# Weight chunks whose low parts come from an accumulating transfer, in a two-layer decoder trunk

## The chip, the cores and the metric

One core of one Trainium2 chip runs the whole program. The metric is the device time of one execution in microseconds (us). Before the change it is 446.27 us, the median of three runs (446.05 to 446.99).

## The reference

`reference` sends x (256 rows of 1024 numbers) through two layers, each closed by `x <- LayerNorm(alpha * x + sublayer(x))`:

```python
h = x @ w_in                                            # layer 0: retention and latent attention
rq, rk, rv, rg, mq, mkv, mkr, mg = _split(h, EVEN_SPLITS)
o_r = head_group_norm(retention_chunkwise(q_r, k_r, _heads(rv, RET_HEADS)))
ret_out = (_merge(o_r) * jax.nn.silu(rg.astype(jnp.float32))).astype(x.dtype)
q_m = rms_norm(mq, q_norm_g) @ w_uq                     # heads are split off in between
kv = rms_norm(mkv, kv_norm_g) @ w_ukv
o_m = causal_attention(q_full, k_full, v_m, (MLA_NOPE + MLA_ROPE) ** -0.5)
return jnp.concatenate([ret_out, mla_out], axis=-1) @ w_out
...
h = x @ w_in                                            # layer 1: block-sparse attention
return (_merge(o) * jax.nn.silu(g)) @ w_out
```

All of it is float32. There are 4 retention heads, 8 latent-attention heads and 16 heads in layer 1, and nearly all of the arithmetic is in the products with the weights.

## The kernel before

**Three matrix multiplications for one.** A float32 product is made of fast multiplications on rounded operands. Each operand is split into a high part, the operand rounded, and a low part, the rest. `mm3` (L169 to L173) then multiplies high by high (L171), low by high (L172 or L173, by which operand comes first) and high by low. The names of parts end in _h or _hi and in _l or _lo.

**Weight chunks.** The weights are cut into 138 chunks in the order in which they are used (`PLAN`); this text counts them from 0, as the code's `state["u"]` does. `fetch` (L190) loads the next chunk from the queue of SP (L195) into a buffer called raw, one of a ring of four, and `load` (L200) has it split by `wsplit` (L204) and `split_to` (L175): ScalarE (ACT in the profile) writes the high part w_h by a copy that rounds (L176), and VectorE (DVE) writes the low part w_l = raw - w_h (L177). There are six buffers for w_h and six for w_l, and raw is free again when the subtraction is done. Chunks 0 to 8 also carry columns of x, transposed, and four of these lie in the ring, five in other buffers. From chunk 9 on nearly all are 128x1024 (512 KB). GpSimd (POOL) does only a few powers for the norms.

**Order.** The order of TensorE (PE) is written out by hand, as tasks that are put between the products of the weights. The other engines stand in an order that a scheduler worked out when the program was built. A load counts its landing on one of eight counters (DMAHW0 to DMAHW7) that are given out in turn, and an instruction that issues a transfer first waits until the counter's previous transfer has landed. Two loads that are not of weights are issued from ACT's queue between its copies for the first chunks (L280): the constants cs, and the retention decay, called decay.

**Places that the prediction speaks of.** Chunk 5 is one of the first nine, whose products go to pm. Chunk 16 is a value chunk of the first retention head (pv). Chunks 88 to 93 lie around the end of the last gate product of layer 0 (pg, gated by L423 and L424 into rgate) and the start of its output projection (acc). The high part of chunk 93 lies in a buffer of its own, w_rqk_h. Chunk 104 is a value chunk of layer 1 (pvo). Chunks 136 and 137 are the last two, of the output projection of layer 1; around them the attention of the last heads is finished: ppt (L566) holds probabilities transposed by PE, which ACT and DVE split into pT_h and pT_l for the product poc, and cog (L840) is the gated result, split into oT_h and oT_l for the output projection acc.

Of the kernel before, what the change touches and what calls it, by code (L numbers as in the profile page):

```python
# [9 lines left out]
F32 = mybir.dt.float32  # L10
F32R = mybir.dt.float32r
BF16 = mybir.dt.bfloat16
I32 = mybir.dt.int32
AF = mybir.ActivationFunctionType
OP = mybir.AluOpType
AX = mybir.AxisListType

P = 128
S = 256
NT = S // P  # L20
DM = 1024
# [10 lines left out]
WBUFS = 6  # L32
# [10 lines left out]
VAL = 1, 2, 1, 1  # L43
LAT1, LAT2, QR = 5, 1, 7
WARM = 9

OFF = np.cumsum([0, 1024, 1024, 2048, 2048, 256, 256, 64, 1024])
O_RQ, O_RK, O_RV, O_RG, O_MQ, O_MKV, O_MKR, O_MG = [int(v) for v in OFF[:8]]
# [106 lines left out]
def trunk(ctx, tc, x, lng, lnb, w, cst, dec, out):  # L155
    nc = tc.nc
    cp = ctx.enter_context(tc.tile_pool(name="const", bufs=1))
    wp = ctx.enter_context(tc.tile_pool(name="weights", bufs=1))
    even = ctx.enter_context(ExitStack())
    wk = even.enter_context(tc.tile_pool(name="even", bufs=1))  # L160
# [5 lines left out]
    def at(name):  # L166
        return ps.tile([P, 512], F32, name=name, tag="at", bufs=4)
# [7 lines left out]
    def split_to(hi, lo, src):  # L175
        done = nc.scalar.activation(hi, src, AF.Copy)  # L176
        nc.vector.tensor_tensor(lo, src, hi.bitcast(F32), op=OP.subtract)  # L177
        return done

    def split(src, shape, name, pool=None, tag=None, bufs=1):  # L180
        pool = pool or wk
        tag = tag or name
        hi = pool.tile(shape, F32R, name=name + "_h", tag=tag + "_h", bufs=bufs)
        lo = pool.tile(shape, F32R, name=name + "_l", tag=tag + "_l", bufs=bufs)
        split_to(hi, lo, src)
        return hi, lo

    state = {"u": 0, "off": 0, "tick": 0}

    def fetch(name, extra=0, home=None):  # L190
        tag, _, ks, cols = PLAN[state["u"]]
        assert tag == name, (tag, name)
        n = len(ks) * len(cols) + extra
        raw = wk.tile([P, n], F32, name="raw", tag=home) if home else wp.tile([P, n], F32, name="raw", tag="raw", bufs=4)
        nc.sync.dma_start(raw, bass.AP(tensor=w.tensor, offset=w.offset + state["off"], ap=[[n, P], [1, n]]))  # L195
        state["u"] += 1
        state["off"] += n * P
        return raw, n, ks, cols

    def load(name, tags=None, raw=None):  # L200
        raw, n, ks, cols = raw or fetch(name)
        return ks, [t.rearrange("p (k c) -> p k c", c=len(cols)) for t in wsplit(raw, n, tags)]

    def wsplit(raw, n, tags):  # L204
        if not tags:
            return split(raw, [P, n], "w", wp, "w", WBUFS)
        hi, lo = [wk.tile([P, n], F32R, name="w_" + t, tag=t) for t in tags]
        split_to(hi, lo, raw)
        return hi, lo
# [36 lines left out]
    pidle = at("pidle")  # L246
    for _ in range(WARM):
        nc.tensor.matmul(pidle, idle[:, :P], idle, start=True, stop=True)
# [21 lines left out]
    xn = [cp.tile([P, DM], F32, name=f"xn{t}") for t in range(NT)]  # L270
    homes = [None] * 4 + [n + e for n in ("rqk", "mqk", "rv") for e in ("_h", "_l")]
    first = [fetch("m", 0 if i == 1 else S, homes[i]) for i in range(KD + 1)]
    for i, (raw, n, ks, cols) in enumerate(first):
        k = ks[0]
        if i != 1:
            at_act = split_to(xT_hi[:, k, :], xT_lo[:, k, :], raw[:, :S])
            for at_k, dst, src in ((2, cs, cst), (4, decay, dec)):
                if k == at_k:
                    with tc.issue_after(at_act.ins):
                        nc.scalar.dma_start(dst, src)  # L280
        wv = wsplit(raw[:, n - len(cols):], len(cols), None)
        for i2 in range(len(cols) // 288):
            j = max(i2, int(i == 1))
            for t in range(NT):
                mm3(pm[t][j][:, :288], x_rows(k), wv, lambda z: z[:, t * P:(t + 1) * P],
                    lambda z: z[:, i2 * 288:(i2 + 1) * 288], start=k == 0, stop=k == KD - 1)
# [19 lines left out]
    for bits in (2.0 ** -2, 2.0 ** -5, 2.0 ** -15, 2.0 ** -22):  # L306
        c = math.floor(rest / bits) * bits
# [89 lines left out]
    def block_proj(name, lhs, tiles, nk=KD):  # L397

        done = 0
        while done < nk:  # L400
            ks, wv = load(name)
            for i, k in enumerate(ks):
                for t in range(NT):
                    mm3(tiles[t], lhs(k), wv, lambda z: z[:, t * P:(t + 1) * P], lambda z: z[:, i, :],
                        start=done == 0, stop=done == nk - 1)
                done += 1
            tick()

    def blockT_proj(name, o):

        ov = o.rearrange("p (c s) -> p c s", c=2)
        for _ in range(2):
            ks, wv = load(name)
            for i, k in enumerate(ks):
                for c in range(2):
                    mm3(ov[:, c, :], wv, x_rows(k), lambda z: z[:, i, c * P:(c + 1) * P], lambda z: z,
                        start=k == 0 and c == 0, stop=k == KD - 1)
            tick()
# [21 lines left out]
    def retention(h, mid=None):  # L440
# [3 lines left out]
        for _ in range(KD // 2):  # L444
            ks, wv = load("qk")
            for i, k in enumerate(ks):
                for c in range(4):
                    mm3(v4[c // 2][:, c % 2, :], wv, x_rows(k), lambda z: z[:, i, c * P:(c + 1) * P],
                        lambda z: z, start=k == 0 and c % 2 == 0, stop=k == KD - 1)
            tick()  # L450
# [331 lines left out]
    wk = ctx.enter_context(tc.tile_pool(name="odd", bufs=1))  # L782
# [87 lines left out]
    for n in range(len(held), 8):  # L870
        if "turned" in state:
            with tc.issue_after(state.pop("turned").ins):
                ks, wv = load("v")
        else:
            ks, wv = load("v")
# [3 lines left out]
    for i in range(2):  # L879
        hi, lo = [wk.tile([P, NT, 512], F32R, name=f"cv{i}_{e}") for e in "hl"]  # L880
# [79 lines left out]
```

## Time and profile before

| | |
|---|---|
| median of three runs | 446.27 us |
| the profiled execution: its time / its span | 447.49 us / 445.7 us |
| PE busy with matrix multiplications / loading weights | 436.2 us (98%) / 389.9 us (87%) |
| DVE busy | 329.9 us (74%) |
| ACT busy | 247.3 us (55%) |
| POOL busy | 10.9 us (2%) |
| mean granted clock of PE | 0.945 of full speed |
| weights' queue: bytes, share of the 16 DMA engines' span | 70.66 MB, 49.6% |
| chain of work that ended last | PE 92%, DVE 3%, ACT 2%, DMA 1%, issue 1% |

The span runs from the first instruction to the last. An engine's busy time is the time in which one of its instructions runs, and it says nothing by itself about whether another engine waits for it: that is read from the waits and from single instructions in the timeline.

### The profile page before, as it was taken

How to read it: one execution, taken by the hardware profiler on the slowest of the kernel's cores; microseconds unless marked ns; L12 is line 12 of the kernel's file. 1: busy time of each engine (PE TensorE's matmuls, PEld its weight loads, DVE VectorE, ACT ScalarE, POOL GpSimd, SP SyncE). 2: the span in 40 equal slices, each digit the busy share in tenths (PEclk: the TensorE clock that was granted, in tenths of full speed). 3: DMA queues.
4: the chain of work that ended last, by engine and by line, in shares of the span. 5: the costliest groups of instructions: out<-in, count | busy, mean ns of one | idle time of the engine just before them, and what ended most of it. 6: DMA issues, size and time to landing. Idle time of an engine off the chain costs nothing.

```text
span 445.7 us, 7654 instructions
## 1 busy us (share of the span) xinstructions
PE 436.2 (98%) x2959; PEld 389.9 (87%) x2959; DVE 329.9 (74%) x586; ACT 247.3 (55%) x439; POOL 10.9 (2%) x18
## 2 busy tenths in 40 slices
PE   8999999999999999999999999999999999999993
PEld 6998899988998888889998888888899999999883
DVE  4889789785876866556488569668767698889747
ACT  5777456663556543345465755503645868595810
POOL 0020000000000000000000000000000000000001
PEclk9999999999999999999999999999999999999997
DMA  8977545454463566554646557922866354634002
GB/s 283 347 242 246 188 143 183 148 168 141 143 188 109 181 203 220 162 189 145 211 142 189 178 176 226 304 63 85 273 207 190 97 169 125 185 96 137 1 1 94
DMA packets 21780, 75.55 MB, mean 170 GB/s; under 512 B 2416, under 2 KB 2800, under 8 KB 21744
## 3 DMA queue, kind: packets, MB, share of 16 engines
q1 hardware_dynamic: 20304, 70.66, 49.6%
q10 hardware_dynamic: 1440, 4.41, 2.9%
q8 instruction: 23, 0.38, 0.3%
q14 instruction: 13, 0.11, 0.1%
HBM read 74.01 MB, written 1.05 MB: 168 GB/s over the span
## 4 chain that ended last, share of the span: by engine, by line
PE 92%; DVE 3%; ACT 2%; DMA 1%; issue 1%; SPq 0%; DVEq 0%; ACTq 0%
PE pg L171 5%; PE pg L172 5%; PE pg L173 5%; PE pj L171 4%; PE pv L171 3%; PE pj L172 3%; PE pj L173 3%; PE pv L173 3%; PE pv L172 3%; PE acc L171 3%; PE acc L172 3%; PE acc L173 3%; PE pa L172 3%; PE pa L173 3%; PE pa L171 2%; PE pq L171 2%
## 5 line engine op out<-in xcount | busy, mean ns | idle before, releaser
L177 DVE TENSOR_TENSOR w_l<-raw,w_h 128x1024 fp32r<-128x1024 f32 (+3 forms) x134 | 156.4, 1170 | 55.1 <-ACT w_h L176 53.7
L176 ACT ACTIVATE w_h<-raw 128x1024 fp32r<-128x1024 f32 (+3 forms) x134 | 135.5, 1015 | 94.9 <-PE pa L172 19.3
L171 PE MATMUL pj<-xT_hi,w_h 128*128 128x256 f32 x128 | 36.1, 282 | 0.0
L172 PE MATMUL pj<-xT_hi,w_l 128*128 128x256 f32 x128 | 35.8, 279 | 0.0
L173 PE MATMUL pj<-xT_lo,w_h 128*128 128x256 f32 x128 | 35.7, 279 | 0.0
L171 PE MATMUL pv<-w_h,xT_hi 128*128 128x512 f32 x64 | 25.7, 402 | 0.0
L171 PE MATMUL pg<-w_h,xT_hi 128*128 128x512 f32 x64 | 25.7, 402 | 0.0
L172 PE MATMUL pg<-w_h,xT_lo 128*128 128x512 f32 x64 | 25.3, 395 | 0.0
L172 PE MATMUL pv<-w_h,xT_lo 128*128 128x512 f32 x64 | 25.3, 395 | 0.0
L173 PE MATMUL pv<-w_l,xT_hi 128*128 128x512 f32 x64 | 25.3, 395 | 0.0
L173 PE MATMUL pg<-w_l,xT_hi 128*128 128x512 f32 x64 | 25.2, 395 | 0.0
L171 PEld LDWEIGHTS pj<-xT_hi,w_h 128*128 128x128 f32 x128 | 24.0, 188 | 0.5
L172 PEld LDWEIGHTS pj<-xT_hi,w_l 128*128 128x128 f32 x128 | 24.0, 188 | 0.0
L173 PEld LDWEIGHTS pj<-xT_lo,w_h 128*128 128x128 f32 x128 | 24.0, 187 | 0.0
L171 PE MATMUL pq<-xT_hi,w_h 128*128 128x256 f32 x64 | 18.3, 286 | 0.0
L171 PE MATMUL pg<-xT_hi,w_h 128*128 128x256 f32 x64 | 18.1, 283 | 0.0
L171 PE MATMUL pmg<-xT_hi,w_h 128*128 128x256 f32 x64 | 18.1, 282 | 0.0
L171 PE MATMUL pkk<-xT_hi,w_h 128*128 128x256 f32 x64 | 18.0, 281 | 0.0
L173 PE MATMUL pmg<-xT_lo,w_h 128*128 128x256 f32 x64 | 17.9, 279 | 0.0
L173 PE MATMUL pkk<-xT_lo,w_h 128*128 128x256 f32 x64 | 17.9, 279 | 0.0
L172 PE MATMUL pq<-xT_hi,w_l 128*128 128x256 f32 x64 | 17.9, 279 | 0.0
L173 PE MATMUL pq<-xT_lo,w_h 128*128 128x256 f32 x64 | 17.9, 279 | 0.0
(302 smaller groups left out, 1239.1 us busy)
## 6 DMA issues: line engine op xcount, KB each, us to landing
raw<-w SPq DMA_DIRECT2D x125, 512.0 KB, 3.8
raw<-w SPq DMA_DIRECT2D x7, 416.0 KB, 7.1
raw<-w SPq DMA_DIRECT2D x4, 256.0 KB, 2.7
xn<-x ACTq DMA_DIRECT2D x2, 512.0 KB, 4.2
decay<-dec ACTq DMA_DIRECT2D x1, 512.0 KB, 7.2
decay_ln<-lng ACTq DMA_DIRECT2D x1, 512.0 KB, 4.1
rv_h_ln<-lnb ACTq DMA_DIRECT2D x1, 512.0 KB, 3.7
lng_ln<-lng ACTq DMA_DIRECT2D x1, 512.0 KB, 4.0
```

The lines of the kernel that those rows point to most:

```text
L171: nc.tensor.matmul(o, ca(a[0]), cb(b[0]), start=start, stop=False, skip_group_check=True)
L172: nc.tensor.matmul(o, ca(a[1]), cb(b[0]), start=False, stop=False, skip_group_check=True)
L173: state["mm"] = nc.tensor.matmul(o, ca(a[0]), cb(b[1]), start=False, stop=stop, skip_group_check=True)
L176: done = nc.scalar.activation(hi, src, AF.Copy)
L177: nc.vector.tensor_tensor(lo, src, hi.bitcast(F32), op=OP.subtract)
```

## The change

For every fourth chunk from chunk 16 on that has 1024 columns and takes the ordinary buffers (26 of the 138: 16, 20, 28, 32, 36, 44, 48, 52, 56, 60, 64, 72, 80, 84, 88, 92, 100, 104, 108, 112, 116, 120, 124, 128, 132, 136), DVE no longer subtracts. ACT writes two copies of raw, the high part and its negative (into the low part's buffer), and a transfer issued by POOL adds raw onto the negative, which leaves raw - w_h there. The ring of raw has five buffers in place of four, and the program reserves 4096 bytes for descriptors of such transfers.

```diff
+BY_DMA = 14, 4
...
-        raw = wk.tile([P, n], F32, name="raw", tag=home) if home else wp.tile([P, n], F32, name="raw", tag="raw", bufs=4)
+        raw = wk.tile([P, n], F32, name="raw", tag=home) if home else wp.tile([P, n], F32, name="raw", tag="raw", bufs=5)
...
     def load(name, tags=None, raw=None):
+        u = state["u"]
         raw, n, ks, cols = raw or fetch(name)
-        return ks, [t.rearrange("p (k c) -> p k c", c=len(cols)) for t in wsplit(raw, n, tags)]
-
-    def wsplit(raw, n, tags):
+        by_dma = not tags and n == DM and u >= BY_DMA[0] and u % BY_DMA[1] == 0
+        return ks, [t.rearrange("p (k c) -> p k c", c=len(cols)) for t in wsplit(raw, n, tags, by_dma)]
+
+    def wsplit(raw, n, tags, by_dma=False):
+        if by_dma:
+
+            hi, lo = [wp.tile([P, n], F32R, name="w_" + e, tag="w_" + e, bufs=WBUFS) for e in "hl"]
+            nc.scalar.activation(lo, raw, AF.Copy, scale=-1.0)
+            nc.scalar.activation(hi, raw, AF.Copy)
+            nc.gpsimd.dma_start(lo, raw, accum_op=OP.add)
+            return hi, lo
...
-    nc = bacc.Bacc("TRN2", target_bir_lowering=False, num_devices=1)
+    nc = bacc.Bacc("TRN2", target_bir_lowering=False, num_devices=1, dynamic_dma_scratch_size=4096)
```

In the changed kernel the line numbers of `split_to` and `fetch` are larger by one, those behind `wsplit` by ten. The order of PE's 2959 matrix multiplications and of SP's loads stays as it was. DVE has 26 subtractions fewer, ACT 26 copies more, and POOL 26 transfers between its powers. The scheduler also moved other things, of which three places follow.

**First place, the loads of the first chunks in ACT's order.** xT_hi is the high part of a chunk's columns of x, w_h that of its weights. Before:

```order
L176 ACTIVATE xT_hi<-raw 128x256 [waits DMAHW4_49]
L176 ACTIVATE w_h<-raw 128x576
L176 ACTIVATE xT_hi<-raw 128x256 [waits DMAHW5_49]
L280 DMA decay<-dec 128x1024 [waits DMAHW6_49]
L176 ACTIVATE w_h<-raw 128x576
L176 ACTIVATE xT_hi<-raw 128x256
```

Now:

```order
L177 ACTIVATE xT_hi<-raw 128x256 [waits DMAHW4_49]
L177 ACTIVATE w_h<-raw 128x576
L177 ACTIVATE xT_hi<-raw 128x256 [waits DMAHW5_49]
L290 DMA decay<-dec 128x1024 [waits DMAHW7_49]
L177 ACTIVATE w_h<-raw 128x576
L177 ACTIVATE xT_hi<-raw 128x256 [waits DMAHW6_49]
```

The order is the same, but the load of decay has another counter: it waits for the transfer that last used DMAHW7, which is the load of chunk 7, where it waited for that of chunk 6 on DMAHW6. (Chunk 9's load no longer waits for DVE, since the ring has a fifth buffer, and the counters came to be given out in another order.)

**Second place, the loads around chunk 93 in SP's order**, with buffer numbers; the fourth row of each is chunk 93. Before:

```order
L195 DMA raw_3011<-w 128x1024 [waits DMAHW2_49,DVE_49]
L195 DMA raw_3029<-w 128x1024 [waits DMAHW3_49,DVE_49]
L195 DMA raw_3047<-w 128x1024 [waits DMAHW4_49,DVE_49]
L195 DMA raw_3065<-w 128x1024 [waits DMAHW5_49,DVE_49]
L195 DMA raw_3071<-w 128x1024 [waits DMAHW6_49,DVE_49]
```

Now:

```order
L196 DMA raw_3026<-w 128x1024 [waits DMAHW0_49,DMASW5_49]
L196 DMA raw_3044<-w 128x1024 [waits DMAHW2_49,DVE_49]
L196 DMA raw_3062<-w 128x1024 [waits DMAHW3_49,DVE_49]
L196 DMA raw_3081<-w 128x1024 [waits DMAHW4_49,DMASW6_49,Activation_49]
L196 DMA raw_3087<-w 128x1024 [waits DMAHW5_49,DVE_49]
```

Chunk 93 took over the buffer of chunk 89, which DVE released by its subtraction; with five buffers it takes that of chunk 88, which is released by ACT's copies and by the landing of the accumulating transfer (DMASW6).

**Third place, the last two chunks in ACT's order.** Before:

```order
L176 ACTIVATE oT_h<-cog 128x256 [waits DVE_49] x2
L176 ACTIVATE w_h<-raw 128x1024 [waits DMAHW0_49,PE_49]
L176 ACTIVATE w_h<-raw 128x1024 [waits DMAHW1_49,PE_49]
L176 ACTIVATE pT_h<-ppt 128x384 [waits PE_49] x4
L176 ACTIVATE oT_h<-cog 128x256 [waits DVE_49] x2
```

Now:

```order
L177 ACTIVATE oT_h<-cog 128x256 [waits DVE_49] x2
L212 ACTIVATE w_h<-raw 128x1024 [waits DMAHW0_49,PE_49]
L211 ACTIVATE w_l<-raw 128x1024 [waits DMASW6_49,PE_49]
L177 ACTIVATE w_h<-raw 128x1024 [waits DMAHW1_49,PE_49]
L177 ACTIVATE pT_h<-ppt 128x384 [waits PE_49] x4
L177 ACTIVATE oT_h<-cog 128x256 [waits DVE_49] x2
```

The negative copy of chunk 136 stands between the high parts of chunks 136 and 137. On DVE the two oT_l and four pT_l around them stay, with one w_l (of chunk 137) between them in place of two.

## Rows read from the trace of the kernel before

**Rows 1.** The page's busy times, and all of PE's longest wait from the waits.

```profile
PE 436.2 (98%) x2959; PEld 389.9 (87%) x2959; DVE 329.9 (74%) x586; ACT 247.3 (55%) x439; POOL 10.9 (2%) x18
...
PE ppt L566 <- DVE pT_l L177: 0.9, 1, 0.9
```

**Rows 2.** Windows, 20 to 400: us, busy PE PEld DVE ACT POOL, clock, DMA, GB/s.

```profile
20.00:400.00 380.00, 380.00 (x2561) 340.70 (x2560) 284.51 (x480) 216.43 (x373) 8.86 (x12) 0.95 0.55 175
```

**Rows 3.** Timeline of ACT, chunk 5: start, us, instruction, [idle before, releaser].

```profile
10.15 0.42 ACT L176 ACTIVATE xT_hi<-raw 128x256 fp32r<-128x256 f32 x1
11.20 0.34 ACTq L280 DMA_DIRECT2D decay<-dec  x1
11.59 0.69 ACT L176 ACTIVATE w_h<-raw 128x576 fp32r<-128x576 f32 x1 [1.02 <-DMA raw<-w]
```

**Rows 4.** Timeline of SP, the first three loads that wait for a counter.

```profile
8.12 0.33 SPq L195 DMA_DIRECT2D raw<-w  x1
9.16 0.33 SPq L195 DMA_DIRECT2D raw<-w  x1
10.19 0.33 SPq L195 DMA_DIRECT2D raw<-w  x1
```

**Rows 5.** Timeline of DVE and PE, chunk 5's low part and its first use.

```profile
12.31 0.76 DVE L177 TENSOR_TENSOR w_l<-raw,w_h 128x576 fp32r<-128x576 f32 x1 [0.96 <-ACT w_h L176]
13.34 0.29 PE L173 MATMUL pm<-w_l,xT_hi 128*128 128x288 f32 x1
```

**Rows 6.** Costly groups by form: count, busy us, mean ns, idle before and releasers.

```profile
L177 DVE TENSOR_TENSOR w_l<-raw,w_h 128x1024 fp32r<-128x1024 f32 x121 | 147.5, 1221 | 52.5 <-ACT w_h L176 51.2 <-PE pvo L173 0.6
L176 ACT ACTIVATE w_h<-raw 128x1024 fp32r<-128x1024 f32 x121 | 127.5, 1057 | 88.8 <-PE pa L172 18.5 <-PE pkk L173 11.6 <-PE pj L173 8.2
```

**Rows 7.** The page's DMA issues: count, KB of each, us from issue to landing.

```profile
raw<-w SPq DMA_DIRECT2D x125, 512.0 KB, 3.8
raw<-w SPq DMA_DIRECT2D x4, 256.0 KB, 2.7
decay<-dec ACTq DMA_DIRECT2D x1, 512.0 KB, 7.2
```

**Rows 8.** Timeline around chunks 88 (first row) and 93 (second row).

```profile
254.25 1.06 ACT L176 ACTIVATE w_h<-raw 128x1024 fp32r<-128x1024 f32 x1 [0.70 <-PE pg L172]
265.28 1.06 ACT L176 ACTIVATE w_rqk_h<-raw 128x1024 fp32r<-128x1024 f32 x1 [0.78 <-DMA raw<-w]
270.45 0.68 DVE L424 SCALAR_TENSOR_TENSOR rgate<-rgate,pg 128x512 f32<-128x512 f32 x1
271.67 0.40 PE L171 MATMUL acc<-w_h,rT_h 128*128 128x512 f32 x1
```

**Rows 9.** Timeline, chunk 104: high part, and first use of the low part.

```profile
311.33 1.06 ACT L176 ACTIVATE w_h<-raw 128x1024 fp32r<-128x1024 f32 x1 [0.49 <-PE pvo L172]
320.68 0.40 PE L173 MATMUL pvo<-w_l,xT_hi 128*128 128x512 f32 x1
```

**Rows 10.** Timeline of ACT, DVE and PE, chunks 136 and 137.

```profile
417.78 1.99 ACT L176 ACTIVATE w_h<-raw 128x1024 fp32r<-128x1024 f32 x2
420.20 1.25 ACT L176 ACTIVATE pT_h<-ppt 128x384 fp32r<-128x384 f32 x3 [0.44 <-PE ppt L566]
...
418.85 2.36 DVE L177 TENSOR_TENSOR w_l<-raw,w_h 128x1024 fp32r<-128x1024 f32 x2 [0.49 <-ACT w_h L176]
421.13 1.48 DVE L177 TENSOR_TENSOR pT_l<-ppt,pT_h 128x384 fp32r<-128x384 f32 x3
...
421.74 0.55 PE L566 MATMUL ppt<-cs,prob 128*128 128x128 f32 x3 [0.90 <-DVE pT_l L177]
426.87 0.40 PE L173 MATMUL acc<-w_l,oT_h 128*128 128x512 f32 x1
```

**Rows 11.** Timeline, chunk 16: high part, and first use of the low part.

```profile
30.47 1.06 ACT L176 ACTIVATE w_h<-raw 128x1024 fp32r<-128x1024 f32 x1
40.73 0.39 PE L173 MATMUL pv<-w_l,xT_hi 128*128 128x512 f32 x1
```

## The prediction

> **What bounds the kernel now.** I read the page's busy times first, then PE's waits, then windows, then single places in the timeline. The busy times put PE at 98% and DVE at 74%; the wait of PE that matters is one of 0.9 us for a pT_l of the last attention [rows 1]. The window from 20 to 400 us decides it: PE is busy for 380.00 of 380.00 us at a granted clock of 0.95, while DVE is busy for 284.51 and ACT for 216.43 [rows 2]. So DVE is not what sets the end. A subtraction that DVE no longer makes is worth nothing unless PE waits for it, and in those 380 us it waits for nothing. What is left to gain lies in the 0.9 us near the end; what can be lost is any place where a weight's part, or a buffer, comes later than PE wants it.
>
> **The change, part by part.** 26 subtractions leave DVE, 26 x 1.221 = 31.7 us of its work, and 26 copies are added on ACT, 26 x 1.057 = 27.5 us [rows 6]. Both lie beside PE's work: ACT would then be busy for about 275 of 446 us, and a chunk is split long before it is used, chunk 16 some 10 us ahead [rows 11]. I cost both at nothing, apart from three places where ACT's or SP's queue is tight. POOL's issues delay only its powers, which stand far apart (8.86 us of work in 380 [rows 2]); at nothing too.
>
> *The head: the load of decay.* This is a side effect of the fifth buffer. In ACT's order (first place above) the load of decay waits for the counter of chunk 6's load, and after the change for that of chunk 7's, one load later. Now ACT stands for 1.02 us and issues decay at 11.20 [rows 3]. SP's own issues, which wait for the earlier loads in the same way, are at 8.12, 9.16 and 10.19 [rows 4], and with 11.20 that is one landing each 1.03 us. So decay is issued at about 12.23, and chunk 5's w_h, right behind it on ACT, moves from 11.59 to 12.62. DVE subtracts right behind that, until 13.07 now and 14.10 then, and PE's first use of the result is at 13.34 [rows 5]: 0.27 us of slack. With 0.03 us for the release to reach PE (w_h ends at 12.28, DVE begins at 12.31 [rows 3, 5]) PE waits 14.13 - 13.34 = 0.79, call it **+0.80 us**. Bounds: nothing, if chunk 7's load has landed when ACT gets there, and 1.03.
>
> *The landing time, L.* I count L from the end of the negative copy to the landing of the transfer that adds onto it. Nothing in this trace is such a transfer. A plain load of 512 KB lands 3.8 us after its issue, one of 256 KB in 2.7 [rows 7], so 256 KB take 1.1 us and what is fixed is 3.8 - 2.2 = 1.6. An addition reads two operands of 512 KB where a load reads one, so I take 1.6 + 2 x 2.2 = **6.0 us** as an estimate. The low end is the plain load, 3.8; less is excluded, since it moves no fewer bytes. The high end is the load of decay, 512 KB beside other loads in 7.2 us [rows 7], and one DVE operation of 1.2 us [rows 6] for an issue that is held up: 8.4. By the Trainium skill (DMA: Bandwidth & Descriptors, Anatomy of one DMA, the path by GpSimd) a transfer takes 2.0 us and its bytes at 436 GB/s, an estimate of 3.2 us for 524,288 bytes; the sum would then be without the next term.
>
> *The output projection of layer 0.* Chunk 93's load takes over the buffer of chunk 88 (second place), which is free only when chunk 88's transfer has landed. Chunk 88's high part begins at 254.25 and takes 1.06 [rows 8]; two copies in a row end some 0.95 apart (two take 1.99 [rows 10], less the first's 1.06 is 0.93), so its negative copy ends at 256.26. The load follows at 256.26 + L, 3.8 later the data is there, and w_rqk_h starts at 256.26 + L + 3.9. Now it starts at 265.28 and has itself waited 0.78 for its load [rows 8]. ACT and DVE go through the gate's copies and products behind it in order, one closely after the other, up to rgate, which ends at 271.13; PE wants the accumulator which that frees at 271.67 [rows 8], 0.54 later. So PE waits for 256.26 + L + 3.9 - 265.28 - 0.54, that is, L - 5.6 within a few hundredths. With L = 6.0 it is **+0.40 us**, from nothing at 3.8 to 2.8 at 8.4.
>
> *The tail.* Between the high parts of chunks 136 and 137 now stands a copy (third place). The pair ends at 417.78 + 1.99 = 419.77 [rows 10]; then chunk 137's would end at 420.72. DVE still has to subtract chunk 137 ahead of the four pT_l. It has one subtraction fewer in front, but ACT's copy is what it waits for: it begins at 420.75, its next operation comes 2.36 - 1.22 = 1.14 later [rows 6, 10], so the first pT_l begins at 421.89 in place of 421.13. PE's wait of 0.90 at 421.74 [rows 10] becomes 1.66: **+0.76 us**. ACT's first pT_h, a third of 1.25 and right behind, would end near 421.14 and is not what is late. All behind it, the last products and the layer norm, shifts with PE. Bounds: nothing if DVE's two subtractions had set it as before, 0.95 for a whole copy.
>
> *Landings that PE waits for itself.* The low part must have landed when PE first uses it. Chunk 104 is nearest: its high part ends at 312.39, the negative copy 0.96 later at 313.35, and PE reads the low part at 320.68 [rows 9], so PE waits for L - 7.3. For chunk 136 the negative copy ends at 419.8 and the use is at 426.87 [rows 10] plus 0.76: L - 7.8. Chunk 16 comes next, 31.53 plus 0.95 against 40.73 [rows 11]: 8.2 if its negative copy comes last, 9.2 if it comes first, as the order has it. At L = 6.0 none costs anything.
>
> *Sum.* 0.80 + 0.40 + 0.76 = 1.96. The profiled execution took 447.49 us, 0.3% above the median, and the terms are differences inside it, so I put them on the median: 446.27 + 1.96 = 448.23, **448.2 us**.
>
> **Rivals.**
>
> *The transfer lands quickly* (L up to 5.6, down to a plain load's 3.8 [rows 7]). Then the output projection costs nothing: 446.27 + 1.56 = 447.8 us. For it speaks that source and destination lie on the chip; against it, that the destination has to be read as well. The skill's 3.2 us would give this time.
>
> *It lands late* (L over 7.3). Then the output projection, chunk 104 and chunk 136 each make PE wait: at L = 8, 447.83 + 2.4 + 0.7 + 0.2 = 451.1 us, at L = 8.4, 447.83 + 2.8 + 1.1 + 0.6 = 452.3 us. For it speaks decay's 7.2 us [rows 7] and that DVE, busy for 75% of the time [rows 2], could hold up POOL. By the Trainium skill (SBUF — State Buffer, Who interferes with whom) GpSimd's writing of descriptors stands still while a copy, cast or scalar operation of DVE holds the port pair that they share; no row here shows it, for POOL issues no transfer before the change.
>
> *Not slower.* The load of decay finds its counter free. ACT gets there once chunk 5's xT_hi is done at 10.57 [rows 3], and if chunks 6 and 7 land close together, the later counter costs at most the 0.27 that are spare [rows 5]. With a quick landing only the tail is left: 446.27 + 0.76 = 447.0 us, which is within 0.2% (0.9 us) of the time before, about what a measurement can tell from no change. It decides from an issue at or before 11.47. Against it: SP's issues are as evenly spaced as landings in turn [rows 4].
>
> *Faster.* If chunk 136's negative copy hardly delays chunk 137's high part, the relieved DVE starts the first pT_l when its pT_h ends, at about 420.62 (420.20 and a third of 1.25 [rows 10]), 0.51 before 421.13; with no wait at the head the time is 445.8 us. That needs a copy of under 0.2 us, against the 1.06 of every one so far [rows 6].
>
> **How the numbers follow.** Forecast (L from 5.6 to 7.3) 0.40; quick landing 0.24; late landing 0.22; not slower 0.10; faster 0.02; the rest 0.02. The forecast's and the quick landing's own range is 447.8 to 449.5 (at 7.3: 1.56 + 1.7). The range runs from 447.2, where no change begins, to 452.3, the high end of L; outside are the cases of not slower and faster, the rest, and the part of the late landing beyond 8.4, about 0.06. Same: 0.10 and half of the rest, 0.11. Faster 0.03 with the other half. Slower 0.86.
>
> **What would show it.** Head: decay's issue near 12.2 and a PE wait of 0.8 for chunk 5's w_l. Projection: w_rqk_h at 256.26 + L + 3.9 and a wait of PE's acc for rgate. Tail: ppt's wait at 1.66. L itself: the page's DMA issues of POOL. DVE's busy time falls to about 298 us, with PE's unchanged. I am wrong if PE's window from 20 to 400 us stays full and ppt's wait is 0.9 or less, or if PE waits for POOL's transfers at chunks other than those named.

## The result, and the profile after the change

The changed kernel takes 449.09 us (median of 4 runs, 448.28 to 449.27) against 446.40 for the kernel before beside it: a ratio of 1.0055, 95% interval 1.0038 to 1.0073. It is slower, by 1.7 to 3.3 us; 448.2 was forecast. Beside 27 runs of the kernel before, in a later comparison, it took 448.90 against 446.85: 1.0040, interval 1.0027 to 1.0053. The profiled execution took 449.27 us, its span 447.5.

The page's busy times, PE's waits by name, and the window of [rows 2]:

```profile
PE 436.0 (97%) x2959; PEld 388.9 (87%) x2959; DVE 300.6 (67%) x560; ACT 270.8 (61%) x465; POOL 33.8 (8%) x44
...
PE ppt L576 <- DVE pT_l L178: 1.7, 1, 1.7
...
PE pm L174 <- DVE w_l L178: 0.7, 3, 0.3
PE pm L172 <- ACT w_h L177: 0.4, 1, 0.4
...
20.00:400.00 380.00, 379.87 (x2560) 340.41 (x2559) 256.99 (x454) 237.55 (x396) 29.94 (x36) 1.00 0.70 209
```

The page now has DVE busy for 29 us less and ACT for 23.5 more, and PE's busy time is what it was. Of the 380 us from 20 to 400 PE now lacks 0.13, where it lacked nothing; most of the loss lies ahead of 20 and behind 400 us, and a late start shows as idle time only in part. PE's order is the same in both kernels, so one can subtract, product by product, the start in the trace before from the start in the trace after. From 9 us on that shift steps up at three places, and nowhere else by more than 0.06:

| place | shift ahead of it | behind it | step | forecast |
|---|---|---|---|---|
| chunk 5 (13.3 us before) | -0.19 | 0.98 | 1.17 | 0.80 |
| acc for rgate (271.7) | 0.72 | 1.11 | 0.39 | 0.40 |
| ppt (421.7) | 0.93 | 1.71 | 0.78 | 0.76 |

Between the places it falls slowly, by 0.27 up to the projection and by 0.18 from there to ppt. The odd one there is the trace before: between this trace and that of the changed kernel's second profiled execution, below, the shift stays within 0.04 from place to place. The profiled execution of before had a granted clock of 0.945 and this one 0.994; that this is the reason is not shown.

**The head**, in the timelines of ACT and PE (now [rows 3, 5]):

```profile
12.31 0.34 ACTq L290 DMA_DIRECT2D decay<-dec  x1
12.69 0.68 ACT L177 ACTIVATE w_h<-raw 128x576 fp32r<-128x576 f32 x1 [2.35 <-DMA raw<-w]
...
13.43 0.40 PE L172 MATMUL pm<-w_h,xT_hi 128*128 128x288 f32 x1 [0.38 <-ACT w_h L177]
13.66 0.29 PE L173 MATMUL pm<-w_h,xT_lo 128*128 128x288 f32 x1
14.22 0.40 PE L174 MATMUL pm<-w_l,xT_hi 128*128 128x288 f32 x1 [0.26 <-DVE w_l L178]
```

ACT stands idle for 2.35 us, decay is issued at 12.31 (forecast 12.23), and PE waits for the high and then for the low part of chunk 5.

**The output projection**, in the timelines of ACT, DVE and PE, and one line of the chain of waits (now [rows 8]):

```profile
255.94 1.05 ACT L211 ACTIVATE w_l<-raw 128x1024 fp32r<-128x1024 f32 x1
...
261.87 4.87 DMA raw<-w
...
266.76 1.06 ACT L177 ACTIVATE w_rqk_h<-raw 128x1024 fp32r<-128x1024 f32 x1 [1.52 <-DMA raw<-w]
...
271.93 0.68 DVE L434 SCALAR_TENSOR_TENSOR rgate<-rgate,pg 128x512 f32<-128x512 f32 x1
...
272.67 0.50 PE L172 MATMUL acc<-w_h,rT_h 128*128 128x512 f32 x1
```

The negative copy of chunk 88 ends at 256.99. Chunk 93's load is issued when the transfer has landed, at 261.87, and takes 4.87, and w_rqk_h begins at 266.76. That is 9.77 us after the negative copy, against the 9.5 (5.6 + 3.9) from which PE was forecast to wait.

**The tail**, in the timelines of ACT, DVE and PE (now [rows 10]):

```profile
418.73 1.04 ACT L212 ACTIVATE w_h<-raw 128x1024 fp32r<-128x1024 f32 x1
419.68 1.04 ACT L211 ACTIVATE w_l<-raw 128x1024 fp32r<-128x1024 f32 x1
420.62 1.04 ACT L177 ACTIVATE w_h<-raw 128x1024 fp32r<-128x1024 f32 x1
...
421.70 1.23 DVE L178 TENSOR_TENSOR w_l<-raw,w_h 128x1024 fp32r<-128x1024 f32 x1 [2.39 <-ACT w_h L177]
422.84 1.48 DVE L178 TENSOR_TENSOR pT_l<-ppt,pT_h 128x384 fp32r<-128x384 f32 x3
...
423.45 0.55 PE L576 MATMUL ppt<-cs,prob 128*128 128x128 f32 x3 [1.69 <-DVE pT_l L178]
```

DVE, relieved of a subtraction, stands idle for 2.39 us because ACT makes the extra copy first; ppt's wait is 1.69 in place of 0.90.

**The landings.** The page's DMA issues (now [rows 7]), and the line of POOL's transfers, duration of an issue in ns and us to landing:

```profile
raw<-w SPq DMA_DIRECT2D x125, 512.0 KB, 4.5
w_l<-raw POOLq DMA_DIRECT2D x26, 512.0 KB, 5.3
...
L213 POOL DMA_DIRECT2D w_l<-raw x26: 859/860/1032, 30.9 to 421.0; - x26
DMA to landing us min/median/max: 4.5/5.3/10.5
```

### The profile page after: what moved, and what is told of

Same layout as the page of the kernel before. It is cut to its first block, busy times and chain, and to the rows that moved or that the text cites. A ratio compares the mean times of both kernels' runs of the same rounds, so it can differ in the third digit from the quotient of the medians.

```text
span 447.5 us, 7729 instructions
## 1 busy us (share of the span) xinstructions
PE 436.0 (97%) x2959; PEld 388.9 (87%) x2959; DVE 300.6 (67%) x560; ACT 270.8 (61%) x465; POOL 33.8 (8%) x44
## 4 chain that ended last, share of the span: by engine, by line
PE 87%; DMA 4%; DVE 3%; ACT 3%; issue 1%; SPq 1%; DVEq 0%; ACTq 0%
PE pg L172 4%; PE pg L173 4%; PE pg L174 4%; PE pj L172 4%; PE pv L172 3%; PE pj L174 3%; PE pj L173 3%; PE pv L173 3%; PE pv L174 3%; DMA raw<-w 3%; PE acc L172 3%; PE acc L173 3%; PE acc L174 3%; PE pa L173 3%; PE pa L174 2%; PE pa L172 2%
## 5 line engine op out<-in xcount | busy, mean ns | idle before, releaser
L178 DVE TENSOR_TENSOR w_l<-raw,w_h 128x1024 fp32r<-128x1024 f32 (+3 forms) x108 | 124.8, 1158 | 65.5 <-ACT w_h L177 64.7
L177 ACT ACTIVATE w_h<-raw 128x1024 fp32r<-128x1024 f32 (+3 forms) x108 | 108.0, 1004 | 62.0 <-PE pa L173 14.9
L213 POOL DMA_DIRECT2D w_l<-raw x26 | 22.7, 873 | 307.5 <-ACT w_l L211 241.0
L211 ACT ACTIVATE w_l<-raw 128x1024 fp32r<-128x1024 f32 x26 | 27.3, 1049 | 11.4 <-PE pmg L173 5.1
L212 ACT ACTIVATE w_h<-raw 128x1024 fp32r<-128x1024 f32 x26 | 27.3, 1050 | 10.1 <-PE pv L173 2.7
L173 PE MATMUL pkk<-xT_hi,w_l 128*128 128x256 f32 x64 | 17.9, 280 | 0.0
```

What stands on the lines that cost most here:

```text
L173: nc.tensor.matmul(o, ca(a[1]), cb(b[0]), start=False, stop=False, skip_group_check=True)
L211: nc.scalar.activation(lo, raw, AF.Copy, scale=-1.0)
L212: nc.scalar.activation(hi, raw, AF.Copy)
L213: nc.gpsimd.dma_start(lo, raw, accum_op=OP.add)
```

## The experiments

The theory under test: the loss is these three places, each made by an order or a buffer, and not a price of transfers and copies as such (the rival). Runs that were taken together share the kernel before: its median is 446.85 us beside the first four experiments, 446.80 beside *Every second chunk from chunk 26 on* and *Four buffers*, and 446.99 beside the other four. Ratios stand with their 95% intervals, whose half-width is 0.4 us at the least, so the size of a single difference is known no better than that.

**The changed kernel again.** No edit.

> The changed kernel itself, once more beside the kernel before. Theory: its loss is three places in which PE waits, read from the two traces as shifts of PE's instructions: 0.98 us at the load of decay, 0.36 at the output projection of layer 0, 0.72 at the tail, together 2.1 us, a ratio of 1.0046. Rival: there is more, because 26 transfers take DMA time and ACT copies on the whole way; then the ratio is 1.006 or more and the shift of PE's instructions grows between the three places.

448.90 us, 1.0040 (1.0027 to 1.0053). The shift again steps at the head (0.90) and at ppt (0.78), and not at the projection. There chunk 93 came earlier, in the timelines of ACT and SP:

```profile
255.20 1.05 ACT L211 ACTIVATE w_l<-raw 128x1024 fp32r<-128x1024 f32 x1
...
261.12 0.33 SPq L196 DMA_DIRECT2D raw<-w  x1
...
265.22 1.06 ACT L177 ACTIVATE w_rqk_h<-raw 128x1024 fp32r<-128x1024 f32 x1 [0.72 <-DMA raw<-w]
```

265.22 less 256.25 is 8.97, under the 9.5. The load was issued 4.87 after the copy's end, about as in the first execution (4.88), but took 4.1 us in place of 4.87. So this term is there in some executions and not in others. Between the places the shift does not grow, which speaks against the rival. It does not either against the trace of the last run below, which has no transfer: 0.18 behind the head, 0.12 ahead of ppt.

**The load of decay two chunks later.**

```diff
-            for at_k, dst, src in ((2, cs, cst), (4, decay, dec)):
+            for at_k, dst, src in ((2, cs, cst), (6, decay, dec)):
```

> One edit of the changed kernel: the load of decay is issued two chunks later in ACT's order, where its counter is free (no wait in the built order). Theory: the head's 0.98 us go and nothing else, so 1.0 us less than the changed kernel, ratio to before 1.0025; chunk 5's w_h begins near 10.6 us, and PE has no wait for it. Rival (the head is late because the fifth buffer moved loads, not because ACT stands): no change against the changed kernel.

447.84 us, 1.0020 (1.0011 to 1.0029): 1.06 us less than the changed kernel by the medians, 0.89 by the two ratios. ACT no longer stands idle ahead of w_h (timeline), and of PE's waits at the head 0.2 us are left, as before the change:

```profile
10.12 0.42 ACT L177 ACTIVATE xT_hi<-raw 128x256 fp32r<-128x256 f32 x1
10.45 0.67 ACT L177 ACTIVATE w_h<-raw 128x576 fp32r<-128x576 f32 x1
...
12.24 0.34 ACTq L290 DMA_DIRECT2D decay<-dec  x1
...
PE pm L174 <- DVE w_l L178: 0.2, 1, 0.2
```

**Chunk 136 split as before.**

```diff
-        by_dma = not tags and n == DM and u >= BY_DMA[0] and u % BY_DMA[1] == 0
+        by_dma = not tags and n == DM and u >= BY_DMA[0] and u % BY_DMA[1] == 0 and u not in (136,)
```

> One edit of the changed kernel: chunk 136 is split by ACT and DVE as before, 25 chunks by transfer. Theory: ppt's wait goes back from 1.69 to 0.9 us, so 0.75 us less than the changed kernel, ratio to before 1.003. Rival (loss in proportion to the transfers): a 26th of 2.1 us, 0.1 us, which cannot be measured.

447.91 us, 1.0023 (1.0014 to 1.0032): 0.99 less by the medians, 0.76 by the ratios. ACT's two copies stand together again, and PE's wait is back at 0.93 (timelines):

```profile
418.57 2.00 ACT L177 ACTIVATE w_h<-raw 128x1024 fp32r<-128x1024 f32 x2
...
422.53 0.55 PE L576 MATMUL ppt<-cs,prob 128*128 128x128 f32 x3 [0.93 <-DVE pT_l L178]
```

**The fifth buffer without any transfer**: the kernel before with the two other parts of the change, `bufs=5` for raw and `dynamic_dma_scratch_size=4096`. Which of the two counts, the run with four buffers below tells.

> The kernel before with the two other parts of the change alone: five chunk buffers and 4096 bytes reserved for descriptors, no chunk by transfer. Theory: the load of decay waits for chunk 7's counter as in the changed kernel, so 1.0 us more than before, ratio 1.0022, with PE's shift complete by 15 us. Rival (the loss comes from transfers and copies): 1.000.

447.67 us, 1.0019 (1.0010 to 1.0028): the head's loss is there with no transfer in the program, and the shift steps by 0.89 at chunk 5. ACT's and PE's timeline:

```profile
11.84 0.34 ACTq L280 DMA_DIRECT2D decay<-dec  x1
12.22 0.68 ACT L176 ACTIVATE w_h<-raw 128x576 fp32r<-128x576 f32 x1 [2.07 <-DMA raw<-w]
...
13.75 0.40 PE L173 MATMUL pm<-w_l,xT_hi 128*128 128x288 f32 x1 [0.26 <-DVE w_l L177]
```

**All three places mended**: decay as above, and chunks 88 and 136 split as before (`u not in (88, 136)`).

> Three edits of the changed kernel at once: the load of decay two chunks later, and chunks 88 and 136 split by ACT and DVE as before; 24 chunks by transfer stay. Theory (all of the loss lies in the three places): as fast as before, ratio 0.9990 to 1.0010, ppt's wait 0.9 us, no wait of PE between 14 and 420 us, and nothing gained though DVE is relieved of 24 x 1.2 = 29 us. Rival (transfers and copies have a price of their own on the whole way): 1.002 or more.

447.12 us against 446.99, 1.0001 (0.9992 to 1.0009). With 24 transfers left in, and 24 subtractions fewer on DVE, the kernel is as fast as before within 0.4 us. One thing in its trace is not understood: from 348 to 358 us the products of pj start 0.113 us apart, where they start 0.118 apart in the traces before and after, without a wait in either, and that gains 0.33 us. It hides no price of the transfers along the way: against the trace of the last run below, which has no transfer, the shift goes from -0.18 at 16 us to -0.20 at 340. No run mends the projection by itself. PE's wait for pT_l and the window of [rows 2]:

```profile
PE ppt L576 <- DVE pT_l L178: 0.9, 1, 0.9
...
20.00:400.00 380.00, 380.00 (x2566) 340.74 (x2565) 258.95 (x459) 238.31 (x397) 29.16 (x36) 1.00 0.69 208
```

**Plain transfers**, which leave the low parts of the 26 chunks at raw itself:

```diff
-            nc.gpsimd.dma_start(lo, raw, accum_op=OP.add)
+            nc.gpsimd.dma_start(lo, raw)
```

> The changed kernel with the 26 transfers as plain copies of raw over the low part: the low parts of those chunks are then not subtracted, so the output differs. It prices the addition. Theory of the prediction (the addition reads a second operand, 1.1 us for each 256 KB): the transfer lands in 5.3 - 2.2 = 3.1 us where the addition takes 5.3. Rival (the addition is hidden behind the writing): 5.3 in both. The time of the kernel stays that of the changed one within 0.4 us by both.

448.48 us, 1.0036 (1.0021 to 1.0050), as the changed kernel. The transfer's landing and issue (page and line):

```profile
w_l<-raw POOLq DMA_DIRECT2D x26, 512.0 KB, 3.9
...
L213 POOL DMA_DIRECT2D w_l<-raw x26: 530/530/692, 32.1 to 421.1; - x26
```

The addition adds 5.3 - 3.9 = 1.4 us to a transfer at the median, and 0.33 to POOL's issue of it. Both expectations missed: it is neither free nor the 2.2 us of a second operand. At the projection w_rqk_h came 9.60 us after the negative copy, and the shift stepped by 0.22, with 4.2 for the landing and 5.3 for the load: it is the load that came late there.

**Every second chunk**, 56 transfers (`BY_DMA = 14, 2`).

> The changed kernel with every second chunk by transfer (from chunk 14 on) instead of every fourth. Theory: the head (0.9 us) and the tail (0.77) are the same places, and the output projection, which hangs on a landing and a load together, loses up to 1 us more since the loads get slower: ratio 1.004 to 1.006. Rival (a price per transfer, here doubled): 1.008 or more, with PE waiting at many chunks.

452.20 us, 1.0106 (1.0088 to 1.0124): more than the theory's 1.006, and what the rival's "1.008 or more" allowed, though not by waits of PE at many chunks, as the rival had it. In the profiled execution (450.61 us) the shift steps at the head and at ppt, and by 1.70 at one new place, 53 us. Four of the six runs took 1.4 to 2.4 us longer than that one, and what they lost was not profiled. The chain of waits there, the timelines of DVE and PE, and windows of that stretch (columns as in [rows 2]):

```profile
41.85 9.34 DMA raw<-w
...
51.30 1.07 ACT w_h L177
...
52.39 1.83 DVE L178 TENSOR_TENSOR w_l<-raw,w_h 128x1024 fp32r<-128x1024 f32 x2 [2.82 <-ACT w_h L177]
...
55.36 0.49 PE L172 MATMUL po<-rv_h,sT_h 128*128 128x512 f32 x1 [1.07 <-ACT sT_h L177]
...
40.00:50.00 10.00, 10.00 (x46) 8.04 (x45) 5.93 (x11) 7.19 (x13) 0.87 (x1) 1.00 1.02 280
50.00:60.00 10.00, 8.83 (x44) 6.89 (x43) 5.83 (x13) 4.34 (x5) 1.52 (x3) 1.00 1.00 313
```

With the DMA engines at a share of 1.0 a load takes 9.3 us and ACT waits for its chunk. DVE's subtractions wait for ACT's copies, the first retention head's scores (sd) stand behind them in DVE's order, and sT_h, for which PE waits, is made from the scores.

**Every second chunk from chunk 26 on**, 51 transfers (`BY_DMA = 26, 2`).

> Every second chunk by transfer, but only from chunk 26 on: 51 transfers in place of 56. Theory: what every second chunk lost over every fourth lies in one stretch, 30 to 60 us, where the loads of the first head and the transfers together fill the DMA engines (share 0.92 to 1.02) and a load takes 9.3 us; with those five left out the ratio falls from 1.0106 to 1.004 to 1.006. Rival (a price per transfer, 51 of 56 remain): 1.009 or more.

449.74 us, 1.0085 (1.0056 to 1.0114; the medians alone give 1.0066, for ten runs spread from 448.10 to 454.07). That lies between what the theory and the rival expected. In the profiled execution (448.95 us) the step at 53 us is gone, and head and ppt are all that is left; from 30 to 60 us the DMA engines are at 0.64, where they were at 0.98 with 56 transfers:

```profile
30.00:60.00 30.00, 30.00 (x150) 24.93 (x149) 25.35 (x48) 18.77 (x29) 1.07 (x2) 1.00 0.64 202
```

So the place was named rightly, but what the longer runs lost was not profiled. A price of many transfers that comes in some executions only stays open.

**Four buffers under the transfers** (`bufs=4` in the changed kernel).

> The changed kernel with four chunk buffers as before; the transfers stay. The load of decay waits for chunk 6's counter again (built order). Theory: the head's 0.9 us are gone, the tail's 0.77 stay, and the fifth buffer was there for a reason: the load four chunks later now waits for a landing. For chunk 108 that is 313.4 (negative copy of chunk 104) + 4.9 (landing) + 4.4 (load) = 322.7 us in place of 317.6, with its own low part at 329.6 against a use near 331.5, so just hidden: ratio 1.002, and up to 1.004 if chunk 96, whose load then waits for chunk 92's landing (about 284 in place of 273.5), comes too late. Rival (head not tied to the buffers): 1.004 with PE's shift of 0.9 us at 13 us.

449.08 us, 1.0044 (1.0028 to 1.0060), above the theory's limit. The head is mended but for 0.21 in the shift, so its loss comes from the fifth buffer and not from the reserved bytes, which are in this kernel too. The tail is not mended (0.79), and the place with sT_h costs 1.59: in the chain of waits a transfer's landing now holds the next load of its buffer.

```profile
42.49 6.10 DMA w_l<-raw
...
48.64 2.57 DMA raw<-w
...
51.32 0.64 ACT w_h L177
...
53.24 0.53 ACT sT_h L177
```

I had looked for this at chunks 96 and 108 and not at the first head. That is what the fifth buffer keeps away.

**The other way round**: the kernel before, four buffers and no transfer, with the subtraction of the last chunk alone moved from DVE to POOL.

```diff
+        return ks, [t.rearrange("p (k c) -> p k c", c=len(cols)) for t in wsplit(raw, n, tags, u in (137,))]
...
+        if by_pool:
+            hi, lo = [wp.tile([P, n], F32R, name="w_" + e, tag="w_" + e, bufs=WBUFS) for e in "hl"]
+            nc.scalar.activation(hi, raw, AF.Copy)
+            nc.gpsimd.tensor_tensor(lo, raw, hi.bitcast(F32), op=OP.subtract)
+            return hi, lo
```

> The kernel before, with the subtraction for the last chunk alone done by POOL instead of DVE; no transfers, four buffers. Theory (the one wait of PE that can be gained is ppt's for pT_l, behind DVE's two subtractions): the first pT_l begins when its pT_h ends, ppt's wait falls from 0.90 to 0.45 us, ratio 0.9990. Rival: POOL is slower than the 7 us that the low part has until its first use, or stands in DVE's way; PE waits there and the ratio is 1.000 or more.

446.53 us against 446.99, 0.9986 (0.9977 to 0.9996): faster than both kernels, and than the kernel before by about as much as ppt's wait got shorter (0.46 us of median, and 0.38 of wait). Timelines of POOL, DVE and PE:

```profile
419.58 2.46 POOL L209 TENSOR_TENSOR w_l<-raw,w_h 128x1024 fp32r<-128x1024 f32 x1 [114.10 <-ACT w_h L208]
...
420.44 1.49 DVE L177 TENSOR_TENSOR pT_l<-ppt,pT_h 128x384 fp32r<-128x384 f32 x3 [0.63 <-ACT pT_h L176]
...
421.05 0.55 PE L572 MATMUL ppt<-cs,prob 128*128 128x128 f32 x3 [0.52 <-DVE pT_l L177]
```

## Why the prediction was right, point by point

*DVE's relief is worth nothing.* Shown to within 0.4 us: 24 subtractions fewer with the three places mended change nothing (1.0001). The one subtraction that PE waits for indirectly, in the tail, has a value, and moving that alone gained.

*The head.* Right in mechanism, and shown from both sides: the fifth buffer makes it without a transfer (+0.82 us of median), and moving the load of decay takes it away (-1.06). The term was sized 0.80 and measured 1.17 in the profiled execution, 0.89 to 1.02 in the profiled ones of six other kernels and runs that have the wait. What was left out: after each of its waits PE's next two products start 0.23 or 0.24 apart (13.43 to 13.66 in the rows), where 0.13 is usual in this stretch, and in this execution the chunks ahead had come 0.19 earlier, which PE lost again.

*The landing time.* The estimate for L was 6.0 us, and at chunk 88 it is 261.87 - 256.99 = 4.9; the median of all is 5.3 and the 0.3 from the copy's end to POOL's issue. What made up for it is the other half of the term: the load behind it took 4.87, where the prediction took the median of all loads, 3.8. The sum, 9.77, is near the 9.9 forecast, by two errors of 1.1 us that cancel, so that the size came out at 0.39 against 0.40 is luck. The load's error was not a price of the transfers. In the trace before this very load was issued at 260.50 (timeline of SP), and ACT waited for it until 265.28 [rows 8]: 4.8 us as well.

```profile
260.50 0.33 SPq L195 DMA_DIRECT2D raw<-w  x1
```

Nor was a transfer under way beside it after the change: chunk 88's had landed, and the next was issued at 276.02. The term was taken from a median where the place itself had a row. It is also less firm than its single number: 0.39 and 0 in two executions of one kernel, since the threshold (9.5 forecast, and 9.77 less the 0.39 is 9.4) lies inside the spread of 8.7 to 9.8 us, in the four profiled executions with this addition that order the loads so. In all four the load was issued 4.9 us after the copy's end; it is the load itself that took from 3.8 to 4.9. At the median over the program, loads did get slower, from 3.8 to 4.5 us, and with five buffers and no transfer they stayed at 3.9.

*The late landing.* The upper bound of 8.4 us did not hold: three landings took 9.6, 9.6 and 10.5 us from their issues (at 320.36, 331.11 and 342.42), and the lower bound of a plain load's 3.8 is no floor either, for the plain transfers of the same bytes landed in 2.9 to 7.1. The long ones cost nothing, as no wait of PE names a transfer; chunk 104, whose slack I had put at 7.3, landed within 5.2. The bound was put on one L for all chunks, where what counts is L at the few with little slack. At each of the three, two or three loads of weights were issued within 0.8 us of the transfer; at the other 23 it was one at most, and those landed in 4.5 to 7.3. With four buffers under the same transfers no such bunch is there, and the longest landing took 7.3. So the bunched loads are the likely cause, though no run changes them alone. By the Trainium skill (DMA: Bandwidth & Descriptors, Anatomy of one DMA) such a transfer takes 3.2 us, an estimate from its fit; the plain ones here took 3.9 at the median, and the adding ones, for which that section has no price, 5.3. By the Trainium skill (SBUF — State Buffer, Who interferes with whom) DVE can hold up the writing of descriptors. Here the longest of 26 issues took 1.03 us and the median one 0.86, and beside the slow landing issued at 320.36 DVE ran nothing until 322.31; whether it held up a part of another landing no view here shows.

*The tail.* Forecast 0.76, measured 0.78 or 0.79 in the shifts of the seven profiled executions that have it, and 0.99 us of median (0.76 by the ratios) when undone. The rival in which the relieved DVE starts pT_l earlier failed for the reason given: the copy takes its full time on ACT, in front.

*The sum.* The steps add up to 2.34 us, or 2.15 with the 0.19 of the head's earlier start taken off, against 1.96 forecast; less the 0.45 by which the shift falls between the places, that leaves the shift of 1.7 behind ppt. The spans differ by 1.8, and the two comparisons of medians say 2.7 and 2.05. The profiled execution of before was at 447.49 itself some 1.1 above its median; so the medians are further apart than the two traces.

## What to carry to other kernels

Before relieving an engine, look whether anyone waits for it: 24 subtractions, 29 us of DVE, beside a PE that is never idle were worth nothing that could be measured, and the one subtraction with a waiter behind it was worth some 0.4 us. What a change of buffers or splitting does to the order of counters and queues can cost more than the work it moves; here an unrelated load, issued from the queue of a busy engine, had come to wait for one transfer more. Where a landing releases a buffer, take landing and next load as one sum, the load at what it took at that very place and not at the median, and compare it with the slack there.

## What the runs showed that was not expected

An accumulating transfer of 512 KB within the chip's SBUF landed in 5.3 us at the median, a plain one in 3.9, and POOL took 0.86 and 0.53 us to issue them. With 56 of them the median landing rose to 6.5 us and that of the weights' loads to 5.7:

```profile
raw<-w SPq DMA_DIRECT2D x125, 512.0 KB, 5.7
w_l<-raw POOLq DMA_DIRECT2D x56, 512.0 KB, 6.5
```

POOL subtracts 128x1024 in 2.46 us, DVE in 1.22.
